# Another order of the DeltaNet projections, and the triangular inverses moved behind all of the preparation

## The chip, the cores and the metric

The kernel runs on one core of one Trainium2 chip. Its engines work side by side and wait for each other through semaphores: PE multiplies matrices, DVE, ACT and POOL work elementwise on 128 partitions, and SP issues most of the DMA transfers. The metric is the time of one execution on the device, in microseconds (us), and the median over several executions is what counts.

## The reference

One block of a bidirectional encoder, with 512 tokens and a model width of 1024. Two token mixers run in parallel on the same projection, a gated DeltaNet and a latent attention (MLA). Sigmoid gates merge them, and a mixture of 16 experts follows.

```python
proj = h @ w_in[l]
dn_qkv, dn_z, dn_b, dn_a, c_q, c_kv, k_r, gates = jnp.split(proj, split_at, axis=-1)
y_dn = gated_deltanet_branch(dn_qkv, dn_z, dn_b, dn_a, ...) @ w_o_dn[l]
y_mla = mla_branch(c_q, c_kv, k_r, ...) @ w_o_mla[l]
g_dn, g_mla = jnp.split(jax.nn.sigmoid(gates), N_BRANCHES, axis=-1)
x = x + gt1 * ((g_dn * y_dn + g_mla * y_mla) @ w_out[l])
...
# gated DeltaNet, once forwards and once backwards, 8 heads of 128, chunks of 64 tokens
qkv = jax.nn.silu(centred_depthwise_conv(qkv, conv_w))
q, k, v = jnp.split(qkv, 3, axis=-1)
lower = jnp.where(strict, jnp.einsum('bhnik,bhnjk->bhnij', k_beta, kc) * decay, 0.0)
t_inv = lax.linalg.triangular_solve(eye + lower, eye, left_side=True, lower=True, unit_diagonal=True)
u = t_inv @ v_beta
w = t_inv @ (k_beta * jnp.exp(gc)[..., None])
def step(state, xs):          # 8 steps, one behind the other
    v_new = u_i - w_i @ state
    o_i = qd_i @ state + intra_i @ v_new
    state = state * jnp.exp(gl_i)[..., None, None] + jnp.swapaxes(ks_i, -1, -2) @ v_new
```

## The kernel before, in words

The block runs in stages. Conditioning, the latents and the attention come first, then the DeltaNet part, which this text is about, then the output mixing and the router, and at last the experts, whose weights stream from DRAM.

Every projection of the DeltaNet is made by `proj_tiles`. One tile is one head, or 128 columns of the gates: 24 matmuls of 128x512, because each float32 product is split into high and low parts (`wh`, `wl`) and made as three. ACT makes the high parts and POOL subtracts for the low parts; every `lo_n`-th subtraction goes to DVE instead (L96). The weights come through four `wraw` buffers, which SP loads (L137), or ACT where `fill_q` says so.

The DeltaNet part has five pieces:

1. **Projections of keys and queries.** Each head goes through `conv` (one ACT operation, four on DVE at L660 and L662, then silu on ACT). The keys are also transposed to token order (`to_tok`: four transposes on PE into the one bank `tok`, a scaled copy on ACT into `tk`, a store). Between heads stand pieces of another, small product (`mod_g`).
2. **Decay blocks**, t = 0 to 3: POOL makes `gM`, PE the bank `pjb`, ACT the exponential `Dx`, POOL `Di`, DVE masks `Dx`. PE's products of keys with keys and queries (bank `gkq`) are multiplied into `nA` and `Di` by DVE (L761).
3. **Inverses.** `inverses(ty)`, once for each type of chunk, inverts 128 triangular blocks of 32x32 on DVE, one block in each partition: a run of 31 rows, and for row i a multiply of i*i elements (L783, `pr`) and a reduction (L784, `lanT`). The input goes through DRAM (`nd`) to `pr` and is copied to `nl`; the result goes through DRAM (`td`, `tt`) to `Tbd` and `TtC`.
4. **Projection of values**, written behind `inverses(0)`, each head followed by one tile of the gates' projection (`fill_g`).
5. **Eight steps.** `level(s)` loads a step's operands and completes the inverse by two small groups of products (bank `I`: `I<-TtC,Mb` and `I<-Tbd,Qb`). `step(s, L)` applies it to the values (bank `V`), passes the state `Sst` on (bank `S`) and writes the output. Steps 0 to 3 take type 0, steps 4 to 7 type 1. `inverses(1)` is written ahead of step 2, and DVE runs it behind `inverses(0)`. `fill_g` gives the rest of the gates' projection: a scheduler puts its matmuls where PE would wait, and what is left follows the last step.

The program is written in this order, and the scheduler fixes each engine's order at build time from dependences and priorities. Behind the steps the outputs `o` are normalised on DVE (L1024, L1032 scales), transposed on PE (bank `oT`) and multiplied by w_o_dn, beside the product of the attention's output (`am`) with w_o_mla.

Of the kernel before, what the change touches and what calls it, by code (L numbers as in the profile page):

```python
# [14 lines left out]
OP = mybir.AluOpType  # L15
# [25 lines left out]
def block_kernel(ctx: ExitStack, tc: tile.TileContext, x, c, positions, w_mod, b_mod, g_mix, w_in, conv_w,  # L41
# [87 lines left out]
    lo_eng, lo_n = [0], [3]  # L129
# [93 lines left out]
    p = bank("mm")  # L223
# [453 lines left out]

    for e, base, feat in ((0, 8, kf), (1, 0, qf)):
        for h, ps in proj_tiles(range(128 * base, 128 * base + 1024, 256)):
# [5 lines left out]
            if e == 0:  # L685
                pool.tensor_copy(feat[h], f)
            for _ in range(2):
                next(mod_g, None)
            sq = dp("sq", 512, bufs=4)
# [3 lines left out]
            sqs.append(sq)  # L693
            if e:
                sp.dma_start(kq_d.rearrange("t p (h n) -> p t h n", h=8)[:, :, h, :], kq[h].rearrange("p t s n -> p t (s n)"))
            if e == 0:
                to_tok(kc, 0, h)
                if h == 5:
                    decays()
            if h % 4 < 3:  # L700
# [33 lines left out]
    lanes_ap = lambda td, l0, n=16: td[l0:l0 + n, :].rearrange("l (j i) -> j l i", j=32)  # L734
    FT, FV = 0, 1
    for t in range(4):
# [31 lines left out]
    def inverses(ty):  # L768
# [4 lines left out]
        sp.dma_start(pr, nd_d[ty])  # L773
        dve.tensor_copy(nl[0:64], pr[0:64])
        dve.tensor_copy(nl[64:128], pr[64:128][:, ::-1])
        pool.memset(T, 0.0)
        pool.memset(T[:, 0:1024:33], 1.0)
        sq3 = lambda v: v.rearrange("p (a b) -> p a b", a=32)
        T3, n3 = sq3(T), sq3(nl)
        for i in range(1, 32):  # L780
            pv = pr[:, :i * i].rearrange("p (a b) -> p a b", a=i)
            nb = n3[:, 0:i, i][:, None, :].to_broadcast([128, i, i])
            dve.tensor_tensor(pv, T3[:, 0:i, 0:i], nb, op=OP.mult)  # L783
            dve.tensor_reduce(T3[:, 0:i, i], pv, axis=AX.X, op=OP.add)  # L784
        To, Tt = pr, nl
        dve.tensor_copy(To[0:64], T[0:64])
# [3 lines left out]
        sp.dma_start(td_d[ty], To)  # L790
        sp.dma_start(tt_d[ty], Tt)

    inverses(0)
    lo_n[0] = 6
    for h, ps in proj_tiles(range(2048, 3072, 256), to=lambda n: bank(n, 1, pp_)):
        sl = dp("sq", 512, bufs=4)
        for _ in range(0):
            next(mod_g, None)
        conv(ps, 16 + h, halves(sl))
        to_tok(sl, 1, h, ssq_k[:, :, h])  # L800
        for _ in range(FV):
            next(fill_g)
    pp_.close()
    wm.close()
    dp.close()
    if stop <= 1.5:
        return
    fill_q[0], lo_n[0] = act, 2

# [65 lines left out]
    def step(s, L):  # L875
# [24 lines left out]
        for g in range(2):  # L900
            hs = slice(4 * g, 4 * g + 4)
            pV = v4(bank("V", 1, ps_))
            for h in range(4):
                mm(pV[:, h, :], Tbd[:, 4 * g + h, :], vtok[:, 4 * g + h, :])
            if s < 7:
                v_ = vtok[:, hs, :]
                dve.tensor_tensor(v_, pV, bt[:, ty, t, hs][:, :, None].to_broadcast([128, 4, 128]), op=OP.mult)
            vn = dp("vn", [4, 128], bufs=2)
            for h in range(4):
                act.activation(vn[:, h, :], pV[:, h, :], AF.Copy, scale=col(beta, 4 * g + h))  # L910
            vns.append(vn)
        for g in range(2):
            if s < 7:
# [12 lines left out]
        for g in range(2):  # L926
# [8 lines left out]
            else:  # L935
                dve.tensor_tensor(Qs[g], pI, Qs[g], op=OP.add)
                pool.tensor_tensor(oo, oo, Qs[g], op=OP.add)

    L = level(0)
    for s in range(8):  # L940
        if s == 2:
            inverses(1)
        Ln = level(s + 1) if s < 7 else None
        step(s, L)
        L = Ln
# [712 lines left out]
```

## Time and profile before

| what | us |
|---|---|
| median of 3 runs (lowest, highest) | 1320.69 (1320.46, 1327.38) |
| the profiled execution | 1326.64 |
| its span in the trace | 1324.8 |

The span leaves out 1.84 us of the profiled execution's own time. PE is busy for 1241.3 us of the span, DVE for 689.0, ACT for 480.3 and POOL for 307.7. A time in a row below counts from the span's start. In the trace keys and queries take the stretch from about 218 to 347 us, the decay blocks lie around 347 to 378, the first inverse runs on DVE from 390.74 to 452.6, the second from 457.52 to 517, the steps end near 645, and the experts take the stretch from about 880 to 1310.

### The profile page before, as it was taken

The numbers are of one execution on the slowest core, as the hardware profiler recorded it, in microseconds if no ns is written. First come the engines' busy times: TensorE is split into PE (matmuls) and PEld (weight loads), VectorE is DVE, ScalarE is ACT, GpSimd is POOL, SyncE is SP. The second block draws the span as 40 slices with busy tenths as digits, with TensorE's granted clock in tenths as the row PEclk, the third lists the DMA queues.
The fourth block names the chain that finished last, engine by engine and source line by source line (L and its number), as shares of the span: only waits on it lengthen the run. The fifth ranks groups of instructions, "written<-read, shape, count | busy, mean of one in ns | idle before, by whom it ended". The sixth has DMA issues, their size and how long they took to land.

```text
span 1324.8 us, 18313 instructions
## 1 busy us (share of the span) xinstructions
PE 1241.3 (94%) x6933; PEld 775.3 (59%) x6933; DVE 689.0 (52%) x1312; ACT 480.3 (36%) x991; POOL 307.7 (23%) x259
## 2 busy tenths in 40 slices
PE   5999999999997987999999999699999999999895
PEld 2767777666676765877888777443443343343233
DVE  4587766365679996434587765501321312222125
ACT  4466655456643333444542326520210120120103
POOL 2321200233443451344222332310200020020003
PEclk9999999999998997999999999799999999999998
DMA  9521213744463466567579793599999999999995
GB/s 340 154 60 42 82 48 94 232 148 129 125 184 96 152 170 187 187 172 214 160 247 336 247 322 126 228 368 421 420 421 420 421 420 421 420 421 420 421 415 187
DMA packets 153507, 333.70 MB, mean 252 GB/s; under 512 B 44560, under 2 KB 104158, under 8 KB 128458
## 3 DMA queue, kind: packets, MB, share of 16 engines
q1 hardware_dynamic: 130048, 308.75, 63.6%
q10 hardware_dynamic: 23034, 23.36, 5.7%
q8 instruction: 55, 0.90, 0.3%
q0 software_dynamic: 336, 0.41, 0.1%
q14 instruction: 34, 0.28, 0.1%
HBM read 308.35 MB, written 24.13 MB: 251 GB/s over the span
## 4 chain that ended last, share of the span: by engine, by line
PE 67%; DVE 14%; DMA 10%; ACT 3%; issue 2%; POOL 1%; SPq 0%; DVEq 0%; ACTq 0%; POOLq 0%
PE mm L88 23%; PE wg L88 8%; PE wu L88 7%; PE dnp L88 6%; PE po L88 5%; DMA exw<-in_w_down_dram 3%; DVE pr L783 3%; PE sc L88 2%; DMA exw<-in_w_gate_dram 2%; PE I L88 2%; PE s L88 2%; PE pja L88 2%; DVE lanT L784 2%; DMA exw<-in_w_up_dram 2%; PE S L88 1%
## 5 line engine op out<-in xcount | busy, mean ns | idle before, releaser
L88 PE MATMUL mm<-hT,wh 128*128 128x512 f32 (+1 forms) x672 | 222.5, 408 | 0.0
L96 POOL TENSOR_TENSOR wl<-wraw,wh 128x512 fp32r<-128x512 f32 (+2 forms) x83 | 120.2, 1463 | 262.7 <-ACT wh L99 245.5
L88 PEld LDWEIGHTS mm<-hT,wh 128*128 128x128 f32 (+1 forms) x672 | 124.8, 189 | 44.2 <-issue 10.8
L99 ACT ACTIVATE wh<-wraw 128x512 fp32r<-128x512 f32 (+1 forms) x139 | 87.2, 650 | 139.7 <-PE mm L88 61.5
L88 PE MATMUL mm<-hT,wl 128*128 128x512 f32 (+1 forms) x336 | 135.7, 404 | 1.3 <-DVE wl L96 1.3
L88 PE MATMUL wg<-exw,xe 128*64 128x512 f32 x512 | 121.1, 600 | 3.6 <-DMA exw<-in_w_gate_dram 2.3
L88 PE MATMUL wu<-exw,xe 128*64 128x512 f32 x512 | 119.4, 605 | 1.5 <-DMA exw<-in_w_up_dram 1.5
L96 POOL TENSOR_TENSOR xl<-xs,xh 128x512 fp32r<-128x512 f32 x32 | 40.3, 1276 | 308.1 <-ACT xh L1358 308.0
L1515 DVE TENSOR_TENSOR ye<-dnp,gt 64x512 f32<-64x512 f32 x30 | 20.6, 688 | 133.4 <-PE dnp L88 117.4
L1456 DVE TENSOR_TENSOR xa<-sc,xa 128x512 f32<-128x512 f32 x56 | 38.5, 691 | 87.7 <-PE sc L88 87.7
L88 PEld LDWEIGHTS wu<-exw,xe 128*64 128x64 f32 x512 | 35.1, 138 | 66.4 <-issue 59.0
L88 PEld LDWEIGHTS mm<-hT,wl 128*128 128x128 f32 (+1 forms) x336 | 63.4, 189 | 16.8 <-DVE wl L96 1.7
L88 PEld LDWEIGHTS wg<-exw,xe 128*64 128x64 f32 x512 | 33.5, 136 | 64.7 <-issue 55.3
L96 DVE TENSOR_TENSOR wl<-wraw,wh 128x512 fp32r<-128x512 f32 (+1 forms) x56 | 47.7, 857 | 35.7 <-ACT wh L99 34.8
L783 DVE TENSOR_TENSOR pr<-lanT,nl 128x1 f32<-128x1 f32 (+30 forms) x62 | 57.5, 927 | 1.7
L88 PE MATMUL po<-W,am 128*128 128x512 f32 x192 | 50.1, 405 | 0.6 <-DVE W L96 0.6
L660 DVE SCALAR_TENSOR_TENSOR cv<-mm,vecT,cv 128x510 f32<-128x510 f32 (+1 forms) x32 | 23.9, 748 | 39.7 <-ACT cv L656 39.1
L88 PE MATMUL mm<-am,wh 128*128 128x512 f32 x128 | 40.8, 398 | 0.0
L88 PEld LDWEIGHTS po<-W,am 128*128 128x128 f32 x192 | 34.6, 188 | 10.4 <-issue 1.6
L88 PE MATMUL mm<-oz,wh 128*128 128x512 f32 x128 | 40.3, 397 | 0.0
L1581 POOL TENSOR_TENSOR xa<-xa,late 128x256 f32<-128x256 f32 (+1 forms) x16 | 10.7, 709 | 124.2 <-DMA late<-in_g_final_dram 124.2
L88 PE MATMUL mm<-OG,xh 128*128 128x256 f32 x128 | 34.1, 304 | 2.8 <-DVE OG L1367 2.8
(596 smaller groups left out, 2418.5 us busy)
## 6 DMA issues: line engine op xcount, KB each, us to landing
exw<-in_w_gate_dram SPq DMA_DIRECT2D x64, 1024.0 KB
exw<-in_w_up_dram SPq DMA_DIRECT2D x64, 1024.0 KB
exw<-in_w_down_dram SPq DMA_DIRECT2D x63, 1024.0 KB
wraw<-in_w_in_dram SPq DMA_DIRECT2D x38, 512.0 KB
wm<-in_w_mod_dram SPq DMA_DIRECT2D x32, 512.0 KB
wraw<-in_w_in_dram ACTq DMA_DIRECT2D x16, 512.0 KB
xa<-in_w_mod_dram SPq DMA_DIRECT2D x16, 512.0 KB
kq<-kq_d SPq DMA_DIRECT2D x7, 1024.0 KB
```

The source lines that it names most:

```text
L88: return pe.matmul(o, lhsT, rhs, start=start, stop=stop)
L96: eng.tensor_tensor(o, a, b, op=OP.subtract)
L99: act.activation(hi, src, AF.Copy)
L660: dve.scalar_tensor_tensor(cv[:, -s:], ps[:, :512 + s], w(d), cv[:, -s:], op0=OP.mult, op1=OP.add)
L783: dve.tensor_tensor(pv, T3[:, 0:i, 0:i], nb, op=OP.mult)
L784: dve.tensor_reduce(T3[:, 0:i, i], pv, axis=AX.X, op=OP.add)
L1456: dve.tensor_tensor(y[t][:, c:c + 512], ps, y[t][:, c:c + 512], op=OP.add)
L1515: dve.tensor_tensor(ye[o_, c], ps[64 * q:64 * q + 64, :], gt2[64 * q:64 * q + 64, c], op=OP.mult)
L1581: pool.tensor_tensor(y[t][:, cs], y[t][:, cs], gfin[:, cs], op=OP.mult)
```

## The change

The projections come in the order values, queries, keys. The eight value heads stay in the buffers of `Dx` and `Di` until they are transposed, since their scale comes from the keys. The transposes follow the keys, then the decay blocks, now with one gate tile (`FT`) behind each t. Only then comes `inverses(0)`, followed by ten more gate tiles, with every low part on POOL (`lo_n` 1000). There is one piece of `mod_g` for each head of values, queries and keys, where each key and each query had two. `kq_d` is stored in the keys' loop.

`inverses` becomes a generator that yields after each row. The input `nl` is now copied transposed, so that a row's operand lies contiguous in memory (`n3[:, i, 0:i]`), where it had steps of 128 bytes (`n3[:, 0:i, i]`). Of `inverses(1)` twelve rows come ahead of step 0. The rest comes in six portions, two in each of the steps 0 to 2, each issued behind the multiply that makes the step's `vtok`.

```diff
+    vals = []
+    for h, ps in proj_tiles(range(2048, 3072, 256)):
+        vals.append(dp("val", 512, bufs=4, tag=("Dx", "Di")[h % 2]))
+        conv(ps, 16 + h, halves(vals[h]))
+        next(mod_g, None)
+        if h == 5:
+            decays()
-    for e, base, feat in ((0, 8, kf), (1, 0, qf)):
+    for e, base, feat in ((1, 0, qf), (0, 8, kf)):
...
-            for _ in range(2):
-                next(mod_g, None)
+            next(mod_g, None)
...
-    FT, FV = 0, 1
+    FT = 1
+    for h in range(8):
+        to_tok(vals[h], 1, h, ssq_k[:, :, h])
     for t in range(4):
...
-        dve.tensor_copy(nl[0:64], pr[0:64])
-        dve.tensor_copy(nl[64:128], pr[64:128][:, ::-1])
+        sq3 = lambda v: v.rearrange("p (a b) -> p a b", a=32)
+        flip = lambda v: sq3(v).rearrange("p a b -> p b a")
+        dve.tensor_copy(sq3(nl)[0:64], flip(pr)[0:64])
+        dve.tensor_copy(sq3(nl)[64:128], flip(pr)[64:128][:, ::-1, ::-1])
...
-            nb = n3[:, 0:i, i][:, None, :].to_broadcast([128, i, i])
+            nb = n3[:, i, 0:i][:, None, :].to_broadcast([128, i, i])
             dve.tensor_tensor(pv, T3[:, 0:i, 0:i], nb, op=OP.mult)
             dve.tensor_reduce(T3[:, 0:i, i], pv, axis=AX.X, op=OP.add)
+            yield i
...
-    inverses(0)
-    lo_n[0] = 6
-    for h, ps in proj_tiles(range(2048, 3072, 256), to=lambda n: bank(n, 1, pp_)):
-        sl = dp("sq", 512, bufs=4)
-        for _ in range(0):
-            next(mod_g, None)
-        conv(ps, 16 + h, halves(sl))
-        to_tok(sl, 1, h, ssq_k[:, :, h])
-        for _ in range(FV):
-            next(fill_g)
...
-    fill_q[0], lo_n[0] = act, 2
+    lo_n[0] = 1000
...
+                done = dve.tensor_tensor(v_, pV, bt[:, ty, t, hs][:, :, None].to_broadcast([128, 4, 128]), op=OP.mult)
...
+            if s < 3:
+                with tc.issue_after(done.ins):
+                    upto_i(INV[s][g])
...
+    for _ in inverses(0):
+        pass
+    for _ in range(10):
+        next(fill_g)
+    fill_q[0], lo_n[0] = act, 2
+
+    INV, inv = ((18, 20), (23, 25), (28, 32)), inverses(1)
+
+    def upto_i(n):
+        while next(inv) < n:
+            pass
+
+    upto_i(12)
     L = level(0)
     for s in range(8):
-        if s == 2:
-            inverses(1)
```

The gates' projection has 24 tiles, so 576 matmuls. Before, 279 of them stand on PE ahead of the first step's products, 139 among the steps and 158 behind the last step. With the change 392 stand ahead of them: 86 between the last key's matmuls and the last `pjb`, then 306 in one run up to the first `I<-TtC`. 157 stand among the steps and 27 behind them.

Three places of the engines' orders follow. First PE at the end of the preparation, where `val` is a kept value head, `ident` the identity of a transpose, and `pja<-hT` is a matmul of a value projection. Before:

```order
L88 MATMUL gkq<-kq_2088 64x128 x2
L88 MATMUL pjb<-gM,Lbd_2045 128x512
L88 MATMUL pja<-hT_97,wh 128x512
L88 MATMUL pja<-hT_97,wl 128x512
L88 MATMUL pja<-hT_98,wh 128x512 x2
L88 MATMUL pjb<-gM,Lbd_2059 128x512
L88 MATMUL pja<-hT_98,wl 128x512
```

Of the change:

```order
L668 MATMUL tok<-ident,val 128x128 x4
L88 MATMUL pjb<-gM,Lbd_2045 128x512
L668 MATMUL tok<-ident,val 128x128 x8
L88 MATMUL pjb<-gM,Lbd_2059 128x512
L88 MATMUL gkq<-kq_2081 64x128 x2
L88 MATMUL gkq<-kq_2082 64x128 x2
L88 MATMUL gkq<-kq_2083 64x128 x2
L88 MATMUL gkq<-kq_2084 64x128
L668 MATMUL tok<-ident,val 128x128 x4
L88 MATMUL gkq<-kq_2084 64x128
```

The decay blocks stood among value projections; they now stand among the values' transposes, which write the one bank `tok` eight times, with 27 gate matmuls in between, all of them ahead of the third transposed head.

Second SP's queue around the first inverse, from just ahead of its load `pr<-nd` to the loads of its result. Before:

```order
L137 DMA wraw<-in_w_in_dram 128x4x256 x2
L773 DMA pr<-nd_2022 128x1024
L137 DMA wraw<-in_w_in_dram 128x4x256 x2
L771 DMA nd_2023<-nA_2034 32x16x32 x4
L137 DMA wraw<-in_w_in_dram 128x4x256 x8
L790 DMA td_2024<-pr 128x1024
L791 DMA tt_2026<-nl 128x1024
L773 DMA pr<-nd_2023 128x1024
L828 DMA TtC<-tt_2026 32x32x32 x4
```

Of the change:

```order
L137 DMA wraw<-in_w_in_dram 128x4x256 x2
L779 DMA pr<-nd_2022 128x1024
...
L137 DMA wraw<-in_w_in_dram 128x4x256 x2
L849 DMA ibd<-int_d 64x8x64 x2
...
L849 DMA ibd<-int_d 64x8x64 x2
L798 DMA td_2024<-pr 128x1024
L799 DMA tt_2026<-nl 128x1024
L779 DMA pr<-nd_2023 128x1024
L842 DMA Tbd<-td_2024 32x8x32
L827 DMA TtC<-tt_2026 32x32x32 x4
L842 DMA Tbd<-td_2024 32x8x32 x11
```

Two weight loads stand right ahead of `pr<-nd` as before, now of gate weights. Of the ten that stood between it and `td`, four are left (two of them between the `nd` stores that the dots leave out), and the loads of steps 0 and 1 stand there instead.

Third DVE at the first two steps, with `pr` and `lanT` the inverse's rows and `vtok` the hand on to the next step's state. Before:

```order
L783 TENSOR_TENSOR pr<-lanT,nl 128x961
L784 TENSOR_REDUCE lanT<-pr 128x31
L786 COPY pr<-lanT 64x1024
L787 COPY pr<-lanT 64x1024
L788 COPY nl<-lanT 64x1024
L789 COPY nl<-lanT 64x1024
L907 TENSOR_TENSOR vtok<-V,bt 128x512 x2
```

Of the change:

```order
L906 TENSOR_TENSOR vtok<-V,bt 128x512
L790 TENSOR_TENSOR pr<-lanT,nl 128x441
L791 TENSOR_REDUCE lanT<-pr 128x21
L790 TENSOR_TENSOR pr<-lanT,nl 128x484
L791 TENSOR_REDUCE lanT<-pr 128x22
L906 TENSOR_TENSOR vtok<-V,bt 128x512
L790 TENSOR_TENSOR pr<-lanT,nl 128x529
L927 TENSOR_TENSOR Sst<-Sst,S 128x4x128
L791 TENSOR_REDUCE lanT<-pr 128x23
L927 TENSOR_TENSOR Sst<-Sst,S 128x4x128
```

The whole second inverse stood ahead of the first `vtok`; its rows now stand between the steps' own operations.

## Rows read from the trace of the kernel before

**Rows 1.** The page: the chain that ended last, by engine.

```profile
PE 67%; DVE 14%; DMA 10%; ACT 3%; issue 2%; POOL 1%; SPq 0%; DVEq 0%; ACTq 0%; POOLq 0%
```

**Rows 2.** Busy time in stretches: PE, PEld, DVE, ACT, POOL, granted clock, DMA share, GB/s.

```profile
215.00:690.00 475.00, 447.90 (x3014) 336.30 (x3014) 307.48 (x571) 219.53 (x508) 167.72 (x137) 0.96 0.58 170
...
525.00:645.00 120.00, 118.01 (x1426) 97.12 (x1426) 52.89 (x111) 55.74 (x183) 46.53 (x39) 0.97 0.63 178
645.00:690.00 45.00, 45.00 (x202) 36.23 (x202) 31.43 (x82) 23.35 (x52) 13.38 (x10) 1.00 0.65 210
...
404.00:434.00 30.00, 23.26 (x93) 18.25 (x92) 29.27 (x36) 10.36 (x24) 11.29 (x8) 0.89 0.31 95
...
518.00:536.00 18.00, 17.94 (x156) 14.66 (x158) 1.58 (x3) 8.41 (x24) 1.11 (x2) 0.60 0.30 80
```

**Rows 3.** PE's waits, 360 to 545 us: total us, times, longest.

```profile
PE tok L668 <- ACT sq L663: 10.9, 4, 5.2
PE S L88 <- DVE vtok L907: 8.0, 1, 8.0
PE gkq L88 <- DVE Di L761: 2.2, 1, 2.2
```

**Rows 4.** PE's timeline: start, us, instruction, idle before it with its releaser.

```profile
403.39 0.63 PE L88 MATMUL mm<-hT,wh 128*128 128x512 f32 x2
...
404.10 0.64 PE L88 MATMUL pjb<-hT,wh 128*128 128x512 f32 x2
406.27 0.66 PE L668 MATMUL tok<-ident,sq 128*128 128x128 f32 x4 [1.54 <-ACT sq L663]
```

**Rows 5.** DVE's timeline in the two inverses; last the page's group of all 62 multiplies.

```profile
395.72 1.16 DVE L783 TENSOR_TENSOR pr<-lanT,nl 128x49 f32<-128x49 f32 x1
...
450.35 1.12 DVE L788 COPY nl<-lanT 64x1024 f32<-64x1024 f32 x1
...
457.52 0.69 DVE L774 COPY nl<-pr 64x1024 f32<-64x1024 f32 x1 [2.11 <-DMA pr<-nd]
...
464.29 0.26 DVE L783 TENSOR_TENSOR pr<-lanT,nl 128x49 f32<-128x49 f32 x1
464.58 0.21 DVE L784 TENSOR_REDUCE lanT<-pr 128x7 f32<-128x49 f32 x1
...
488.24 1.23 DVE L783 TENSOR_TENSOR pr<-lanT,nl 128x576 f32<-128x576 f32 x1
489.50 0.76 DVE L784 TENSOR_REDUCE lanT<-pr 128x24 f32<-128x576 f32 x1
...
L783 DVE TENSOR_TENSOR pr<-lanT,nl 128x1 f32<-128x1 f32 (+30 forms) x62 | 57.5, 927 | 1.7
```

**Rows 6.** SP's queue: issues with their start and length, and one wait.

```profile
452.61 0.34 SPq L791 DMA_DIRECT2D tt<-nl  x1
453.88 0.32 SPq L773 DMA_DIRECT2D pr<-nd  x1
467.24 19.39 SPq L828 DMA_DIRECT2D TtC<-tt  x4
...
SPq L828 <- DMA wraw<-in_w_in_dram: 29.2, 3, 13.0
```

**Rows 7.** ACT's timeline (one row), then groups by line: count, busy us, mean ns.

```profile
425.93 1.14 ACT L674 ACTIVATE tk<-tok,ssq_k 128x128 f32<-128x128 f32 x4 [0.68 <-PE tok L668]
...
L744 ACT ACT_TABLE_LOAD x2 | 2.6, 1283 | 0.0
...
L745 POOL TENSOR_TENSOR Di<-Dx,Mpk 128x512 f32<-128x512 f32 x6 | 8.5, 1422 | 1.2 <-ACT Dx L744 1.2
```

**Rows 8.** Groups on DVE behind the steps, 640 to 780 us.

```profile
L96 DVE TENSOR_TENSOR am<-a__6132,am 128x512 fp32r<-128x512 f32 x1 | 0.7, 693 | 1.5 <-ACT am L99 1.5
...
L1024 DVE SCALAR_TENSOR_TENSOR sqo<-o 128x128 f32<-128x128 f32 x24 | 7.4, 370 | 0.0
...
L1032 DVE TENSOR_TENSOR o<-o,ssq 128x1024 f32<-128x1024 f32 x4 | 6.8, 1768 | 0.0
```

More of the change, by code (lines that the diff above doesn't have):

```diff
@@ L693, in block_kernel @@
             sqs.append(sq)
-            if e:
+            if e == 0:
                 sp.dma_start(kq_d.rearrange("t p (h n) -> p t h n", h=8)[:, :, h, :], kq[h].rearrange("p t s n -> p t (s n)"))
-            if e == 0:
                 to_tok(kc, 0, h)
-                if h == 5:
-                    decays()
             if h % 4 < 3:
@@ L773, in inverses @@
         sp.dma_start(pr, nd_d[ty])
-        dve.tensor_copy(nl[0:64], pr[0:64])
-        dve.tensor_copy(nl[64:128], pr[64:128][:, ::-1])
+        sq3 = lambda v: v.rearrange("p (a b) -> p a b", a=32)
+        flip = lambda v: sq3(v).rearrange("p a b -> p b a")
+        dve.tensor_copy(sq3(nl)[0:64], flip(pr)[0:64])
+        dve.tensor_copy(sq3(nl)[64:128], flip(pr)[64:128][:, ::-1, ::-1])
         pool.memset(T, 0.0)
         pool.memset(T[:, 0:1024:33], 1.0)
-        sq3 = lambda v: v.rearrange("p (a b) -> p a b", a=32)
         T3, n3 = sq3(T), sq3(nl)
@@ L791, in inverses @@
         sp.dma_start(tt_d[ty], Tt)
-    inverses(0)
-    lo_n[0] = 6
-    for h, ps in proj_tiles(range(2048, 3072, 256), to=lambda n: bank(n, 1, pp_)):
-        sl = dp("sq", 512, bufs=4)
-        for _ in range(0):
-            next(mod_g, None)
-        conv(ps, 16 + h, halves(sl))
-        to_tok(sl, 1, h, ssq_k[:, :, h])
-        for _ in range(FV):
-            next(fill_g)
+        yield 32
     pp_.close()
@@ L906, in step @@
                 v_ = vtok[:, hs, :]
-                dve.tensor_tensor(v_, pV, bt[:, ty, t, hs][:, :, None].to_broadcast([128, 4, 128]), op=OP.mult)
+                done = dve.tensor_tensor(v_, pV, bt[:, ty, t, hs][:, :, None].to_broadcast([128, 4, 128]), op=OP.mult)
             vn = dp("vn", [4, 128], bufs=2)
```

## The prediction, before the result was known

> **What bounds the kernel now.** I read the chain of the last end first. PE holds 67% of it, DVE 14%, DMA 10% [rows 1], so the time is PE's work and the places where PE waits for DVE. Then the stretches. From keys to output mixing, 215 to 690 us, PE is busy for 447.90 of 475 us, which leaves 27.1 us idle at a mean granted clock of 0.96 [rows 2]. PE's waits say where: 10.9 us in four waits for a value head (`sq`) that the transposes need, 8.0 us in one wait of the state products for `vtok`, 2.2 us for `Di` [rows 3]. The first two have one cause. DVE runs the inverses beside the convolutions and ahead of the first `vtok`, so what PE needs stands in DVE's queue. A wait costs more than its length. After the 8.0 us one, PE is busy for all of 518 to 536 us at a granted clock of 0.60, between the two levels of 1.2 and 2.4 GHz, and around the value waits, 404 to 434, the mean is 0.89 [rows 2]. Behind the steps PE has no idle time: 45.00 of 45 us at 1.00 [rows 2], because 158 gate matmuls lie there.
>
> The experts' stream starts only when the mixing and the router are done. A microsecond won or lost between 215 and 690 us therefore goes to the end in full.
>
> **What goes.** Idle time: 27.1 us, of which some 2.5 us are short waits at places that stay (decays, `vn`), so 24.6. Slow clock: 18 us at 0.60 is 7.2 us lost, 30 us at 0.89 is 3.3, and the rest I put at 1.5, since 0.04 of 475 us is 19 us, an upper bound that counts idle stretches too [rows 2]: 12.0. Together **36.6 us**. PE's own work stays the same, 576 gate matmuls included; a matmul takes 0.236 us (three in 0.71 [rows 4]).
>
> **A shorter inverse.** From 49 to 576 elements the multiply grows by 0.97 us, or 1.84 ns an element, the reduction beside it by 0.55 us, or 1.04 ns [rows 5]. The multiply's operand has steps of 128 bytes, the reduction's input none. Contiguous, I take the reduction's rate. All squares from 1 to 31 are 10416 elements, so 0.80 ns each is 8.3 us; the input copies become strided like those of the result, 1.12 for 0.69 us [rows 5], two of them, minus 0.9. Gain: 7.4 us on DVE for each inverse; lower bound nothing, if the multiply is slow for its two inputs instead.
> The Trainium skill ("SBUF — State Buffer", Door 1: The DMA port swizzle) says that memory is read in 16-byte lines and a stride is free up to four float32. The 1.84 against 1.04 ns agree with it.
> Undisturbed, an inverse takes now about 47 us: multiplies 31 x 0.17 + 10416 x 1.84 ns = 24.4, reductions 15.8, copies 4.9, gaps 2. All 62 multiplies took 57.5 us [rows 5], 8.7 more than 2 x 24.4, so some 4.4 us for each inverse are disturbance. New: 47 - 7.4 + 4.4 = **44 us**.
>
> **The new end of preparation.** Eight transposes of values now pass through one `tok` bank: 0.66 us on PE [rows 4], then 1.14 us on ACT [rows 7], and the next may not start before. 27 gate matmuls lie between the first three, so two or three round trips are covered by them and some by `pjb` and `gkq`; I count two as bare, 2.4 us. ACT changes its function table on the way, twice 1.28 [rows 7], 2.6. The last decay chain (`Dx` on ACT, `Di` 1.42 on POOL [rows 7], masks on DVE) has nothing beside it for 3.2, estimated from its rows. Sum 8.2 idle, and 2 for the clock behind it, as around the value waits: **10.2 us**. Bounds: 2.2, what the wait for `Di` costs now [rows 3], and 14. Storing `kq_d` in the keys' loop and one `mod_g` piece fewer per head cost nothing: the projections' 24 matmuls per head (5.7 us) cover both; without that cover a store's issue would be some 0.4 us per head.
>
> **First inverse under 306 gate matmuls.** The run takes 306 x 0.236 = 72.2 us. The chain beside it: two weight loads stand ahead of `pr<-nd` on SP and wait for buffers, freed about 34 matmuls into the run, 8.0, and a split, so 10; `pr<-nd` to the copy 3.6 (453.88 to 457.52 [rows 5, 6]); inverse 44; `tt` to DRAM like that load, 3.6; issue of four `TtC` loads 1.9 and their landing 3.6. That is 66.7, ahead of PE by 5.5 us. I put **1 us** for it, 0 to 4.
> The price if SP is not free: before, `TtC` loads waited for weight loads, 29.2 us in three waits, and ended their issue at 486.63, 34.0 us after `tt` was issued [rows 6]. The change takes eight of those loads off SP's queue there, and I take the short end.
>
> **Steps 0 to 3 with portions of the second inverse.** Rows 13 to 31 are 9766 elements, at 2 x 1.05 ns and 0.4 us a row some 28 us, with input, copies and weights 32. DVE is busy for 52.89 of 120 us in the steps now [rows 2], so in the 79 us of steps 0 to 3 some 35 + 32 = 67 of 79 us: it fits, narrowly. The 8.0 us wait disappears, but each state sum and `vtok` may find a row in progress, at most 1.2 us for a multiply of 961. Six portions at 0.75: **4.5 us**, 0 to 9. The steps 4 to 7 need `TtC` of type 1 only some 14 us after the last portion; nothing for it.
>
> **Behind the last step.** Only 27 gate matmuls are left there, and 59 matmuls on `am` can follow before the transposes `oT`: 86 x 0.236 = 20.3 us of PE. DVE must by then have done `sqo` 7.4, 17 operations of 0.69 (splits of `am` and weights, products, sums) 11.7, and the scalings of `o` 6.8 [rows 8]: 25.9. The transposes come 5.6 us late, the first `am` split 1.5 us [rows 8], and the clock behind it 2.6, like around a wait of 5.2 us now. **9.7 us**, 3 to 13; before it was 0.
>
> **Sum.** 10.2 + 1 + 4.5 + 9.7 = 25.4 new against 36.6 gone: 11.2 us less. The profiled execution took 1326.64 us, its span 1324.8 and 1.84 around it, so it would be 1315.4. It stands 5.95 us above the median of 1320.69; the same difference from the median gives **1309.5 us**. About 0.5%, 6.6 us, is what a measurement of this kernel can tell from no change: 1314.1 to 1327.3.
>
> **Rivals.**
> 1. *The seams cost their upper bounds.* End of preparation 14, first inverse 4, portions 9, transition 13: 40 us, and nothing is won: 1324. For it: the value transposes did stall PE four times before, through ACT and DVE [rows 3]. Against it: those waits were for DVE, which is now idle there. No measurable change, 1314 to 1327. Chance 0.25.
> 2. *The scheduler's order hides the seams.* End of preparation 2.2, inverse 0, portions 4.5, transition 6: 12.7, so 1296.8. For it: 24 gate tiles give much freedom. Against it: few of them are left at either seam. 1296 to 1303. Chance 0.12.
> 3. *The other side: the first result's loads wait on SP as before.* With 34.0 us from `tt` to the last `TtC` issue [rows 6] in place of 5.5, the chain takes 95.2 us, 23 us more than the run of matmuls, and the stretch behind it runs slow, 7.2 us more [rows 2]: 1309.5 + 29 = 1338.7. Slower than can be measured once the chain is some 17 us longer than worked out: 5.5 us ahead, then 11.6 of stall, then the clock. For it: weight loads by ACT now fill the same buffers. Against it: SP's own queue is nearly empty there. Chance 0.08.
> 4. *The first inverse runs beside POOL's subtractions.* The change gives POOL all low parts. A multiply of 49 elements took 1.16 us beside POOL's work and 0.26 alone, the reductions 0.21 [rows 5]. If all 31 multiplies meet one, 28 us in place of 4.4 lie on the chain: 18 us of stall and 7 of clock, 1309.5 + 24 = 1333.7. At half of them it is 14 us, still 4 us late: 1313. From 22 us of disturbance on it is slower. Chance of that 0.05, since most low parts were POOL's before too, at 4.4 us.
> The Trainium skill ("GPSIMD Engine Reference", 1. Specifications) says the same as a rule: POOL shares its memory interfaces with DVE and contends with DVE instructions of two inputs. It speaks against giving POOL all of them; the 1.16 against 0.26 agree.
>
> **How the numbers follow.** As summed, 1303 to 1314: 0.50, likeliest, so 1309.5. Rivals 1 to 4: 0.25, 0.12, 0.08, 0.05. The range 1297 to 1327 leaves out rivals 3 and 4 and the edges, under 2 in 10; the forecast's own range is 1303 to 1314. Faster by over 0.5%: 0.50 + 0.12 = 0.62. Within 0.5%: 0.25. Slower: 0.13.
>
> **What would show it.** In the changed trace: multiplies of 576 elements near 0.77 us; no wait of transposes for `sq` and none of 8 us for `vtok`; PE's run of gate matmuls without a gap up to `I<-TtC`, and `TtC` issued within 10 us of `tt`; waits of a few us at `tok<-val` and at `oT`; a granted clock near 1.00 from 390 to 640 us. The prediction is wrong if PE waits more than 10 us at `I<-TtC`, if the multiply stays at 1.2 us, or if DVE is more than 95% busy in steps 0 to 3.

## The result, and the profile after

The changed kernel takes 1340.38 us (median of 4 runs, 1337.37 to 1341.41) where the kernel before takes 1322.6 in the same runs: a ratio of 1.0135, 95% interval 1.0106 to 1.0164. It is slower by some 18 us. The forecast was 1309.5, with a range of 1297 to 1327. The profiled execution took 1341.41 us, its span is 1339.5, which is 14.7 us longer than that of before. On PE that is 4.2 us more busy time and 10.5 us more idle time. The page's line of the changed kernel:

```profile
PE 1245.5 (93%) x6933; PEld 775.0 (58%) x6933; DVE 677.6 (51%) x1308; ACT 476.8 (36%) x988; POOL 307.9 (23%) x263
```

PE's waits in the changed kernel, with total, count and longest, answer to [rows 3].

```profile
PE mm L88 <- DVE wl L96: 12.4, 3, 8.6
...
PE gkq L88 <- DVE Di L767: 6.5, 3, 3.1
PE tok L668 <- ACT tk L674: 3.9, 3, 1.4
PE oT L1050 <- DVE o L1045: 3.4, 4, 1.7
PE pjb L88 <- ACT Dx L750: 2.8, 2, 1.8
```

Both old waits are gone, that for `sq` (10.9 us) and that of 8.0 us for `vtok`. Five others stand in their place: among the decay blocks (`gkq`, `tok`, `pjb`), for low parts of gate weights (`wl`), and behind the last step (`oT`). The stretches of the changed kernel, with the columns of [rows 2], show where they lie.

```profile
380.00:450.00 70.00, 56.75 (x319) 40.19 (x318) 30.94 (x56) 36.65 (x76) 27.41 (x24) 0.90 0.54 158
450.00:525.00 75.00, 66.38 (x276) 52.18 (x275) 57.80 (x82) 23.73 (x39) 39.98 (x33) 0.95 0.67 202
525.00:645.00 120.00, 114.75 (x1287) 90.81 (x1286) 78.35 (x151) 54.43 (x168) 44.36 (x40) 1.00 0.56 160
645.00:700.00 55.00, 50.22 (x439) 40.32 (x437) 35.80 (x100) 27.17 (x84) 17.73 (x13) 1.00 0.73 228
700.00:760.00 60.00, 56.36 (x247) 45.02 (x248) 49.41 (x64) 16.07 (x27) 13.16 (x8) 0.94 0.86 299
```

The first line holds the end of the preparation: 13.3 us idle at a clock of 0.90. The second holds the first inverse: 8.6 idle at 0.95. The third holds most of the steps, 5.3 idle at 1.00, where before [rows 2] had 2.0 idle but a stretch at 0.60. The fourth holds the end of the steps, which now lies near 676 us, and the transposes of the output, the fifth what follows them: 4.8 and 3.6 idle. Up to 677 us only 0.6 of that is idle. Before, there was none up to 690 [rows 2] and none behind it. The first line below is of the changed kernel, the second of before:

```profile
645.00:677.00 32.00, 31.37 (x364) 26.84 (x363) 15.39 (x33) 13.63 (x49) 10.49 (x9) 1.00 0.75 231
690.00:760.00 70.00, 70.00 (x308) 54.74 (x307) 54.68 (x66) 20.48 (x36) 19.32 (x13) 1.00 0.87 299
```

The mean clock of a stretch counts its idle time too. The slow time itself lies in three places of the changed kernel, each at a granted clock of 0.50, the level of 1.2 GHz:

```profile
424.80:438.50 13.70, 10.82 (x47) 7.01 (x46) 6.83 (x11) 7.72 (x14) 7.55 (x6) 0.50 0.56 133
517.00:523.80 6.80, 2.80 (x7) 2.23 (x8) 4.46 (x6) 0.00 (x0) 3.46 (x4) 0.50 0.60 193
701.30:708.10 6.80, 4.28 (x17) 3.15 (x16) 6.80 (x11) 1.26 (x2) 0.00 (x0) 0.50 0.84 301
```

PE is busy there for 10.8, 2.8 and 4.3 us. If it works at half its speed, as the levels say, these cost 5.4, 1.4 and 2.1 us; this is an estimate.

The end of the preparation as its own timeline shows it, on PE of the changed kernel (start, us, instruction, idle before it):

```profile
412.12 1.13 PE L88 MATMUL pjb<-gM,Lbd 128*128 128x512 f32 x2 [1.85 <-ACT Dx L750]
415.07 0.66 PE L668 MATMUL tok<-ident,val 128*128 128x128 f32 x4 [1.26 <-ACT tk L674]
418.29 1.09 PE L88 MATMUL gkq<-kq 128*64 128x128 f32 x14 [1.54 <-DVE Di L767]
422.52 0.66 PE L668 MATMUL tok<-ident,val 128*128 128x128 f32 x4 [1.32 <-ACT tk L674]
424.52 0.86 PE L668 MATMUL tok<-ident,val 128*128 128x128 f32 x4 [1.35 <-ACT tk L674]
429.07 3.68 PE L88 MATMUL gkq<-kq 128*64 128x128 f32 x32 [1.93 <-DVE Di L767]
...
446.58 2.09 PE L88 MATMUL gkq<-kq 128*64 128x128 f32 x32 [3.05 <-DVE Di L767]
```

Eight waits of 1 to 3 us (one of them in the lines left out) stand in 35 us: the round trips of the one `tok` bank and the chain `pjb`, `Dx`, `Di`, `gkq`, in turn. Then the first inverse on DVE of the changed kernel:

```profile
461.56 0.75 DVE L767 TENSOR_TENSOR Di<-gkq,Di 128x256 f32<-128x256 f32 x2
470.37 1.14 DVE L782 COPY nl<-pr 64x1024 f32<-64x1024 f32 x1 [8.07 <-DMA pr<-nd]
471.52 2.88 DVE L783 COPY nl<-pr 64x1024 f32<-64x1024 f32 x1
...
480.55 1.01 DVE L790 TENSOR_TENSOR pr<-lanT,nl 128x49 f32<-128x49 f32 x1
...
499.95 0.76 DVE L790 TENSOR_TENSOR pr<-lanT,nl 128x576 f32<-128x576 f32 x1
500.75 0.76 DVE L791 TENSOR_REDUCE lanT<-pr 128x24 f32<-128x576 f32 x1
...
519.18 1.03 DVE L797 COPY nl<-lanT 64x1024 f32<-64x1024 f32 x1
520.25 1.29 DVE L96 TENSOR_TENSOR wl<-wraw,wh 128x512 fp32r<-128x512 f32 x2
```

The row operand does what was forecast: 0.76 us for 576 elements, as the reduction beside it, where [rows 5] had 1.23. The Trainium skill ("SBUF — State Buffer", Door 1: The DMA port swizzle) has a stride free only within a 16-byte line; the 0.76 against 1.23 agree. But the inverse begins at 470.37, 79.6 us later than before, and two low parts of gate weights stand behind it on DVE. The next matmul in PE's order needs the first of them, so PE stands from 512.4 on and gets it at 521:

```profile
521.00 0.80 PE L88 MATMUL mm<-hT,wl 128*128 128x512 f32 x1 [8.59 <-DVE wl L96]
...
535.73 0.50 PE L88 MATMUL mm<-hT,wl 128*128 128x512 f32 x1 [1.96 <-DVE wl L96]
...
537.32 0.46 PE L88 MATMUL I<-TtC,Mb 128*32 128x32 f32 x32
```

One more thing shows in PE's own work. The pieces of `mod_g` keep their 64 matmuls but take 16.8 us of PE in place of 10.6. A timeline row and the page's group, first of before, then of the changed kernel:

```profile
240.41 1.06 PE L88 MATMUL mod<-wm,sil 128*32 128x512 f32 x8
L88 PE MATMUL mod<-wm,sil 128*32 128x512 f32 x64 | 10.6, 605 | 0.0
225.81 1.05 PE L88 MATMUL mod<-wm,sil 128*32 128x512 f32 x4
L88 PE MATMUL mod<-wm,sil 128*32 128x512 f32 x64 | 16.8, 605 | 0.0
```

Two pieces that stand side by side (eight matmuls) take as long as one alone (four), and in the changed kernel each stands alone.

### The profile page after: what moved, and what is told of

Its sections match the earlier page's. It is cut to its first block, busy times and chain, and to the rows that moved or that the text cites. A ratio compares the mean times of both kernels' runs of the same rounds, so it can differ in the third digit from the quotient of the medians.

```text
span 1339.5 us, 18333 instructions
## 1 busy us (share of the span) xinstructions
PE 1245.5 (93%) x6933; PEld 775.0 (58%) x6933; DVE 677.6 (51%) x1308; ACT 476.8 (36%) x988; POOL 307.9 (23%) x263
## 5 line engine op out<-in xcount | busy, mean ns | idle before, releaser
L88 PE MATMUL mm<-hT,wh 128*128 128x512 f32 (+1 forms) x800 | 261.2, 406 | 0.0
L96 POOL TENSOR_TENSOR wl<-wraw,wh 128x512 fp32r<-128x512 f32 (+2 forms) x87 | 122.9, 1425 | 285.7 <-ACT wh L99 262.2
L88 PEld LDWEIGHTS mm<-hT,wh 128*128 128x128 f32 (+1 forms) x800 | 148.6, 189 | 50.7 <-ACT wh L99 7.2
L88 PE MATMUL mm<-hT,wl 128*128 128x512 f32 (+1 forms) x400 | 162.3, 406 | 10.6 <-DVE wl L96 10.6
L88 PEld LDWEIGHTS mm<-hT,wl 128*128 128x128 f32 (+1 forms) x400 | 75.3, 188 | 32.8 <-DVE wl L96 11.4
L660 DVE SCALAR_TENSOR_TENSOR cv<-mm,vecT,cv 128x510 f32<-128x510 f32 (+1 forms) x48 | 35.9, 748 | 58.4 <-ACT cv L656 57.8
L96 DVE TENSOR_TENSOR wl<-wraw,wh 128x512 fp32r<-128x512 f32 (+1 forms) x52 | 41.7, 806 | 29.6 <-ACT wh L99 24.2
L790 DVE TENSOR_TENSOR pr<-lanT,nl 128x1 f32<-128x1 f32 (+30 forms) x62 | 43.2, 697 | 1.8
L88 PEld LDWEIGHTS po<-W,am 128*128 128x128 f32 x192 | 34.7, 188 | 10.4 <-issue 1.6
L662 DVE SCALAR_TENSOR_TENSOR cv<-mm,vecT,cv 128x511 f32<-128x511 f32 (+1 forms) x48 | 35.9, 749 | 1.4
```

What stands on the lines that cost most here:

```text
L88: return pe.matmul(o, lhsT, rhs, start=start, stop=stop)
L96: eng.tensor_tensor(o, a, b, op=OP.subtract)
L660: dve.scalar_tensor_tensor(cv[:, -s:], ps[:, :512 + s], w(d), cv[:, -s:], op0=OP.mult, op1=OP.add)
L662: dve.scalar_tensor_tensor(cv[:, :512 - s], ps[:, s:], w(d), cv[:, :512 - s], op0=OP.mult, op1=OP.add)
```

## The experiments

A seam is here a place where PE passes from one piece of the program to the next and may have to wait; cover is other, independent work that PE can do there. The theory after the result, called that of the seams: what the new order costs is cover. Before, the value projections (192 matmuls) lay under the first inverse and the gates' 576 were free for the rest. Now the whole chain from the last key to the output has only the gates' matmuls to hide under, and it got longer at its start. The row operand and the portions are no cause of the loss. Rivals: the portions slow the steps; DVE's low parts alone are the cause; the order costs nothing and a shorter inverse just moves a wait. Medians, and ratios to the kernel before with their intervals; in the runs marked * the scale of the values is left out, so they are no versions to use and only show where time goes:

| kernel | us | ratio |
|---|---|---|
| changed kernel | 1340.38 | 1.0135 (1.0106 to 1.0164) |
| before, contiguous rows | 1307.21 | 0.9893 (0.9867 to 0.9919) |
| before, rows and portions | 1306.12 | 0.9887 (0.9862 to 0.9911) |
| changed, strided rows | 1350.52 | 1.0211 (1.0185 to 1.0238) |
| changed, four more tiles' low parts on POOL | 1345.06 | 1.0171 (1.0146 to 1.0197) |
| changed, second inverse whole | 1342.75 | 1.0142 (1.0118 to 1.0166) |
| changed, no gate tile in the blocks | 1331.45 | 1.0061 (1.0039 to 1.0082) |
| changed, neither queue holds low parts back | 1336.33 | 1.0101 (1.0074 to 1.0128) |
| changed, values transposed at once * | 1323.17 | 1.0006 (0.9992 to 1.0020) |
| changed, these three together * | 1319.19 | 0.9973 (0.9959 to 0.9986) |
| changed, the first two together | 1330.07 | 1.0057 (1.0038 to 1.0076) |
| rows and portions, POOL takes the value stage | 1309.45 | 0.9909 (0.9888 to 0.9930) |
| rows and portions, no scale * | 1305.75 | 0.9877 (0.9855 to 0.9900) |
| three together, 64 matmuls kept back * | 1324.15 | 1.0012 (1.0001 to 1.0022) |
| two together, 64 kept back | 1333.41 | 1.0076 (1.0055 to 1.0096) |
| three together, 59 kept back, all low parts on POOL * | 1319.01 | 0.9968 (0.9950 to 0.9986) |
| two together, 64 kept back, all low parts on POOL | 1334.31 | 1.0096 (1.0079 to 1.0114) |

**One part alone, in the order of before.** The row operand only:

```diff
-        dve.tensor_copy(nl[0:64], pr[0:64])
-        dve.tensor_copy(nl[64:128], pr[64:128][:, ::-1])
+        dve.tensor_copy(sq3(nl)[0:64], flip(pr)[0:64])
+        dve.tensor_copy(sq3(nl)[64:128], flip(pr)[64:128][:, ::-1, ::-1])
...
-            nb = n3[:, 0:i, i][:, None, :].to_broadcast([128, i, i])
+            nb = n3[:, i, 0:i][:, None, :].to_broadcast([128, i, i])
```

> The kernel before with the contiguous row operand alone (order, portions and fill as before). Theory of the seams (the new order costs more at its seams than its cover is worth; the row operand is a gain by itself): both inverses get 7 to 8 us shorter, the 8.0 us wait for vtok falls below 2 us and most of the 7.2 us of slow clock behind it goes, the waits of the transposes shrink from 10.9 to 6 to 9 us: 1302 to 1311 us. Rival, the order was what mattered (a shorter inverse only lets PE wait for something else): 1318 to 1324 us.

And with the second inverse in portions, edited as in the change:

> The kernel before with the contiguous row operand and the second inverse in portions in the steps; the order of the projections, the decay blocks and the fill stay as before. Theory of the seams: as the one with rows alone or up to 6 us better, since the first vtok no longer stands behind the second inverse: 1298 to 1309 us. Rival, the portions slow the steps (a state sum waits for a row each time): 5 to 10 us above the one with rows alone.

Both came out in the theory's range: 1307.21 and 1306.12 us, clearly faster than before. PE's waits with rows and portions in the old order:

```profile
PE tok L668 <- ACT sq L663: 5.8, 4, 2.1
PE gkq L88 <- DVE Di L761: 2.2, 1, 2.2
...
PE S L88 <- DVE vtok L911: 1.1, 1, 1.1
```

and its stretch from keys to output, which has 13.7 us idle at a clock of 1.00, where before it was 27.1 at 0.96:

```profile
215.00:690.00 475.00, 461.31 (x3121) 347.69 (x3122) 311.94 (x600) 227.35 (x520) 165.47 (x141) 1.00 0.62 185
```

These are the waits that the change was forecast to remove, and the old order removes them too, without new ones. Rows alone give nearly all of it: the `vtok` wait falls from 8.0 to 2.2 us there. So from 1306 to 1340, some 34 us are the price of the order and of what goes with it, the lone pieces of `mod_g` among them. The other direction, the strided operand in the changed kernel:

> The changed kernel with the strided row operand of before (that alone undone). Theory of the seams: the first inverse, which nothing else of DVE interrupts, takes 8 us longer and PE waits that much longer ahead of the first step; a part of the longer second inverse shows in the steps: 1347 to 1355 us. Rival, that chain is not what PE waits for: within 3 us of 1340.

1350.52 us, 10 more. The first inverse takes 57.9 us there from its first copy to its last, where the changed kernel has 49.8, and PE's wait for the low part that stands behind it grew from 8.6 to 16.7 us by as much:

```profile
527.61 0.80 PE L88 MATMUL mm<-hT,wl 128*128 128x512 f32 x1 [16.70 <-DVE wl L96]
```

**Portions.** `upto_i(32)` ahead of `level(0)`, nothing in the steps:

> The changed kernel with the second inverse in one piece behind the first on DVE, not in portions. Theory of the seams: the portions are a gain in this order; the first vtok now waits for rows 13 to 31 and the copies of the second inverse, 30 us and more, of which few gate matmuls can cover anything: 1352 to 1372 us. Rival, the portions are what slows the steps: 1325 to 1338 us.

Neither theory had it right. It took 1342.75 us, which the intervals do not tell from the changed kernel. The portions are no cause of the loss, and no gain that can be measured: the first state products wait 6.0 us, not 30, since the scheduler itself puts `vtok` among the rows of an inverse that is written ahead of it.

```profile
551.65 2.08 PE L88 MATMUL S<-vtok,ktok 64*128 64x128 f32 x16 [6.03 <-DVE vtok L906]
```

**Low parts behind the first inverse.** Four more tiles with `lo_n` 1000, behind the ten:

```diff
-    fill_q[0], lo_n[0] = act, 2
+    fill_q[0] = act
+    for _ in range(4):
+        next(fill_g)
+    lo_n[0] = 2
```

> The changed kernel with four more gate tiles whose low parts all go to POOL, so that none of those ahead of the first step stands behind the inverse on DVE. Theory of the seams: PE runs through the gate matmuls and waits for TtC instead, for some 7 to 10 us: 1336 to 1342 us. Rival, the 8.6 and 2.0 us waits for DVE's low parts are the cause: 1327 to 1332 us.

It took 1345.06 us, outside both theories' ranges and within the intervals of the changed kernel, and the edit did not remove the wait: PE waits 8.6 us as before, now for POOL. POOL clears `lanT` for the second inverse, and that waits for the first inverse's last copy; POOL's timeline of the changed kernel shows the clearing already:

```profile
520.28 0.95 POOL L784 MEMSET lanT<- 128x1024 f32 x1 [15.89 <-DVE nl L797]
```

So in addition DVE clears for type 1 (`eng = dve if ty else pool`):

> The changed kernel with four more gate tiles whose low parts all go to POOL, and the clearing of the second inverse's result done by DVE, so that neither queue holds a low part back until the first inverse ends. Theory of the seams: the wait of 8.6 us for a low part goes, and PE waits for TtC instead, 5 to 9 us: 1336 to 1345 us. Rival, those waits are the cause: 1328 to 1332 us.

1336.33 us, 4 less than the changed kernel, though the two intervals overlap. PE was busy for 74.85 of the 75 us up to 525, so the wait itself is gone, and the wait for `TtC` that the theory put in its place did not come; but of its 10.6 us more than half are lost again. Between 645 and 690 PE is idle for 9.5 us, where the changed kernel has 4.8 between 645 and 700. No gate matmul is left behind the last step, where the changed kernel has 27. The longest single wait there, 5.0 us, is for ACT's first high part of `am`, with which the next product begins.

```profile
450.00:525.00 75.00, 74.85 (x318) 59.39 (x314) 58.60 (x82) 24.28 (x40) 43.47 (x33) 0.99 0.66 197
...
645.00:690.00 45.00, 35.51 (x365) 28.94 (x363) 30.09 (x85) 22.08 (x78) 16.42 (x11) 0.89 0.77 242
```

**The end of the preparation.** `FT = 0`, and 14 gate tiles behind the first inverse's start:

> The changed kernel with no gate tile among the decay blocks, and those four tiles behind the first inverse's start instead. Theory of the seams: gate matmuls are a fixed stock, so the blocks' idle time grows by some 4 to 9 us and the stretch under the first inverse gets as much more cover; the blocks' chain also gets shorter by the four tiles' work on ACT and POOL, two table loads of 1.28 us for each: 1330 to 1342 us. Rival, the gate tiles among the blocks carry the stretch: 1348 us and more.

1331.45 us, 9 less, near the low end of the theory's range. But the growth of the blocks' idle time by 4 to 9 us did not come: it is 11.3 us from 380 to 450, where the changed kernel has 13.3. The load `pr<-nd` goes out at 453.69 where the changed kernel has 462.21, and the copy begins at 457.80. So the gate tiles delayed the blocks more than their matmuls covered; that this comes from their work on ACT and POOL was not tested. This run also leaves 64 gate matmuls behind the last step in place of 27. Then `to_tok(vals[h], 1, h)` right behind `conv`, in place of the eight transposes behind the keys:

> The changed kernel with each value head transposed right behind its convolution, without the scale by the keys' norms, which this kernel leaves out. Theory of the seams: the eight transposes no longer lie on the chain from the last key to the first inverse; the decay blocks take 40 us in place of 58, their idle time falls from 13.3 to some 6 us, and the steps end earlier by that and leave more gate matmuls for the last seam: 1320 to 1330 us. Rival, the blocks are slow for another reason, or PE waits as long further on: 1337 to 1343 us.

1323.17 us, 17 less, the largest single part, in the theory's range. `pr<-nd` goes out at 447.33, and PE is busy for 68.24 of the 70 us that had 56.75:

```profile
380.00:450.00 70.00, 68.24 (x370) 48.87 (x369) 42.24 (x74) 41.97 (x62) 37.64 (x32) 1.00 0.52 150
```

The control without the scale in the old order took 1305.75 us against 1306.12, so leaving out the scale is no gain where the transposes lie off the path. In the changed order they lie on it, and without the scale one copy on ACT stands for four scaled ones. A run with the transposes behind the keys but without the scale was not made, so how the 17 us split between place and scale is not shown.

> Control for the runs without the scale: the kernel before with the contiguous row operand and the portions, and the values' transposes copied without the scale by the keys' norms, which this kernel leaves out. If the scale as such costs nothing on the path: within 3 us of 1306. If ACT's three more operations for each head count: 1298 to 1303 us.

**Together.**

> The changed kernel with all three seams taken away together: no gate tile among the decay blocks, no low part held back by the first inverse (POOL makes those of four more tiles, DVE clears the second inverse's result), and each value head transposed at once without the scale by the keys' norms, which this kernel leaves out. Alone they gave 9, 4 and 17 us. Theory of the seams: what the order costs is these seams, so together they give 20 to 30 us and the kernel comes near that with the order of before: 1309 to 1320 us. Rival, the order costs something more (values no longer cover the first inverse): 1320 to 1330 us.

> The changed kernel with no gate tile among the decay blocks and no low part held back by the first inverse; everything is computed. Theory of the seams: 9 and 4 us add up: 1325 to 1331 us. Rival, they are the same wait: 1331 to 1336 us.

1319.19 and 1330.07 us, the first at the edge between the two ranges. The three alone sum to 30 us, together they give 21, which fits one stock of matmuls under which all of them hide. Some 13 us to the control stay. In the trace of the three together PE has no idle time from 450 to 525 us, and 10.4 us from 645 to 690, at a clock of 0.92, where no gate matmul is left. More than half of that is one wait for the first high part of `am`; a run that loads `am` earlier was not made. The last line is of PE's waits from 645 to 700:

```profile
450.00:525.00 75.00, 75.00 (x381) 59.97 (x380) 60.67 (x98) 24.12 (x45) 39.81 (x31) 1.00 0.77 224
645.00:690.00 45.00, 34.55 (x221) 26.99 (x222) 36.75 (x98) 18.24 (x53) 9.06 (x6) 0.92 0.86 290
...
PE mm L88 <- ACT am L99: 5.6, 1, 5.6
```

The pages of the control and of the three together say that idle time is the smaller part of the rest:

```profile
PE 1233.4 (95%) x6933; PEld 768.7 (59%) x6933; DVE 670.7 (51%) x1312; ACT 475.7 (36%) x967; POOL 298.3 (23%) x259
PE 1240.7 (94%) x6933; PEld 772.1 (59%) x6933; DVE 670.3 (51%) x1304; ACT 474.6 (36%) x966; POOL 313.1 (24%) x267
```

The spans differ by 12.0 us, of which 7.3 are PE's busy time and 4.7 its idle time. PE is busy for 3.2 us more in the stretches at a clock of 0.50, which costs 1.6 us by the estimate above. The rest of the 7.3 is PE's own work, here too with `mod` at 18.9 us against 10.6, partly set off by the sums over squares (`pja<-sq,ones`), 10.1 against 13.4. No run with two pieces of `mod_g` side by side in the new order was made.

Would keeping some back for that place help? The tiles ahead of the steps go from 18 to 14:

> The run with three seams taken away (without the scale of the values, which this kernel leaves out), with 14 gate tiles written ahead of the steps in place of 18, so that 64 gate matmuls are left behind the last step where there were none. Theory of the seams: the steps start some 14 us earlier, the idle time and slow clock behind the last step (10.4 and 3.6 us) fall below 5 us, and that is most of what is left: 1306 to 1313 us. Rival, PE waits for the first inverse's result instead, or the order costs something more: 1316 to 1322 us.

> The changed kernel with no gate tile among the decay blocks, no low part held back by the first inverse, and 64 gate matmuls left behind the last step; everything is computed. Theory of the seams: as much better than its pair with none left: 1318 to 1326 us. Rival: the first inverse, which ends later here than without the values' transposes, leaves PE waiting for TtC: 1327 to 1333 us.

1324.15 and 1333.41 us, the first slower than its pair, the second not by its interval. But the edit did one thing more: DVE had a part of the low parts again, with 12.2 us of waits for them in the first. So the same with `lo_n` 1000 for all gate tiles:

> The run with three seams taken away (without the scale of the values, which this kernel leaves out), with 59 gate matmuls left behind the last step and all low parts of gate tiles on POOL. Theory of the seams: no wait for a low part ahead of the steps, and the last seam's 10.4 us idle and slow clock mostly gone: 1306 to 1314 us. Rival, gate matmuls kept back at one end are missed at the other (PE waits for TtC by as much as it gains), or the order costs something more: 1316 to 1322 us.

> The changed kernel with no gate tile among the decay blocks, all low parts of gate tiles on POOL and 64 gate matmuls left behind the last step; everything is computed. Theory of the seams: 1318 to 1326 us. Rival, as above: PE waits for TtC, whose inverse ends 11 us later here than without the values' transposes: 1327 to 1332 us.

1319.01 and 1334.31 us: nothing gained by the one, 4 us lost by the other. The rival was right for the first; the second is even above the rival's range. PE now waits for the first inverse's result, 4.5 us in the first run (and 5.9 in the second), and runs at 0.95 there, and the last stretch still has 5.8 us idle:

```profile
513.18 0.66 PE L88 MATMUL I<-TtC,Mb 128*32 128x32 f32 x32 [4.45 <-DMA TtC<-tt]
```

```profile
450.00:525.00 75.00, 69.50 (x424) 55.12 (x423) 61.82 (x107) 25.74 (x56) 38.15 (x31) 0.95 0.73 207
645.00:690.00 45.00, 39.24 (x206) 31.02 (x206) 31.37 (x88) 22.12 (x58) 11.65 (x9) 0.94 0.65 224
```

Gate matmuls that are kept for one end are missed at the other. That fits a shortage of cover in this order; a run that gave the chain other work to hide under, without changing the order, was not made. How the last 13 us split by cause is therefore not shown, only that PE's own work has a larger part in them than its idle time.

**Beyond both kernels.** Rows and portions in the old order, and all low parts of the value stage on POOL:

> The kernel before with the contiguous row operand, the second inverse in portions, and all low parts of the value stage on POOL instead of five in six. DVE loses some operations of 0.69 us that stand between rows and convolutions, so the remaining 5.8 us of waits for value heads shrink by 1 to 3 us; the rows meet POOL's work more often: 1302 to 1309 us.

1309.45 us, just above its range and 3 above the kernel without this edit; the intervals overlap, so which share is the better one is not shown. The fastest version of everything computed is the old order with rows and portions, 1306.12 us, 1.1% below before; rows alone are as fast within the intervals.

## Why the prediction was wrong, step by step

**What goes, 36.6 us: right as to the places.** Both waits went with the change. But in the old order with rows and portions the stretch's idle time falls by 13.4 us too, and its clock rises from 0.96 to 1.00. The account did not ask what each part of the change would win alone: some 14 us come from the contiguous rows alone, without the new order.

**A shorter inverse: right.** 0.76 us for 576 elements (0.77 forecast). All 62 multiplies take 43.2 us where they took 57.5, so 7.2 us for each inverse (8.3 forecast).

**The new end of preparation, 10.2 us: the first step that failed.** It measured 13.3 us idle and, by the estimate above, 5.4 us in clock: 18.7, beyond its bound of 14. I counted two bare round trips and one decay chain; the trace has three bare round trips, and waits for `Di` at three of the four decay blocks and for `Dx` at two. And I priced only PE's waits there. The same stretch also sets when the first inverse starts: `pr<-nd` goes out 15 us earlier with the values transposed at once and unscaled.

**First inverse under 306 matmuls, 1 us: the second step that failed.** It cost 10.6 us idle (8.59 and 1.96) and 1.4 us in clock, 12.0 in all, beyond its bound of 4. Counted from the last `pjb` at 451.98, `pr<-nd` went out at 462.21, as the 10 us said. The load then took 8.2 us (3.6 forecast) and the inverse 49.8 (44). The 3.6 came from the second inverse's load, which has no weight load right ahead of it; the prediction counted the two weight loads ahead of the first one as a wait for buffers, but not as work that lengthens the load behind them. The issue of the four `TtC` loads ended at 530.82, so 78.8 us after the start where 63.1 was forecast, and against a run of 72.2 us. The wait's place was not foreseen at all: not at `I<-TtC`, but at gate matmuls whose low part stands behind the inverse on DVE. Taking it away gave some 4 us, not clear of noise, and no gate matmul was then left behind the last step.

**Steps, 4.5 us: near in number, by luck.** They have 5.3 us idle up to 645, less the 1.96 us that belongs to the line above, and 0.6 up to 677: 3.9. The price was for waits at rows of the inverse on DVE. The trace has short waits there, most of them for ACT (`vn`, `Qb`, `o`), and hardly any for DVE.

**Behind the last step, 9.7 us: right.** 7.8 us idle from 677 to 760 and 2.1 us in clock: 9.9.

**PE's own work, put as unchanged: the third step that failed.** The prediction had it stay the same, and let one `mod_g` piece fewer per head cost nothing, since the projections' matmuls cover that. But PE has hardly any idle time where the pieces stand (busy for 111.64 of 112 us from 225 to 337), so their own time counts: 16.8 us for 10.6, 6.2 more. The sums over squares and a small product with ones gave back 3.7 of that (12.8 to 10.1 and 2.1 to 1.1). Over the whole span PE is busy for 4.2 us more, although it is busy for 5.7 us less in the stretches at a clock of 0.50 (29.2 us in place of 34.9), worth 2.8 us. So PE's own work grew by some 7 us, an estimate; what makes up the part that `mod` does not explain is not shown.

Sum with what was measured: 18.7 + 12.0 + 3.9 + 9.9 = 44.5 against 36.6, so 7.9 us more. The span grew by 14.7; the rest is PE's own work, the term that stood at nothing.

**What the prediction said would show it.** The multiply came near 0.77 us, the old waits for `sq` and `vtok` went, and waits at `tok<-val` and `oT` came. PE did not wait at `I<-TtC`. Its run of gate matmuls without a gap and a clock near 1.00 from 390 to 640 us did not come, and the issue of `TtC` ended 10.6 us behind `tt`. None of the three signs of being wrong came, so they did not cover the places where the time went.

**The rivals.** The third gave 1338.7, near the result, and for a wrong reason: the issue of `TtC` began 3.0 us after that of `tt` and ended 10.6 us after it, not 34.0. The fourth, the inverse beside POOL, holds in small: 49 elements took 1.01 us again, and the inverse was 5.8 us longer than forecast, not 24. The first, seams at their upper bounds, came nearest in mechanism: its 40 us were 44.5, but not at its places. Two of the four seams passed their bounds and the other two stayed below, and PE's own work it left unchanged too. None of them has the four stretches draw on one stock of 576 matmuls; that fits why the edits together gave 21 of 30 us and why matmuls kept back gained nothing. It does not explain the miss itself, since the sum took each stretch's matmuls rightly from the order: the chains beside them were longer than priced. The chance of 0.13 for a slower kernel was too low.

## What to carry to other kernels

Where one stock of independent work fills several gaps, price the gaps together: what fills one is missing in the next, so count the chain from end to end against the stock. Work that leaves the chain's cover (here 192 matmuls of value projections, some 45 us, moved ahead of it) is then lost stock; this last is argued, no run here tests it. A stretch of short round trips ahead of a long serial piece costs twice, once by PE's own waits and once by the later start. And of a change with several parts, ask for each what it would do in the old kernel: here one edit of the memory layout held nearly the whole gain. And work that is said to cost nothing, since something else covers it, costs its full time where its own engine has no idle time: look at what stands beside it in the order.

## What was not expected of the hardware

A load of the same tile took 8.2 us from issue to use at 462 us and 5.2 at 520.84 (the copy began at 526.04), where [rows 5, 6] have 3.6. The 8.2 stands right behind two weight loads on the queue; without them right ahead, in the run with no gate tile in the blocks, the same load took 4.1 us (453.69 to 457.80).

The transposing copy of 64x1024 elements took 1.14 us in one instruction and 2.88 in the next, which flips the other half, beside POOL's clearings and low parts. Multiplies of 16 to 49 elements, which take 0.2 us alone, took 1.0 to 1.15 each four times in a row. They lie from 476.61 to 481.56, beside POOL's subtractions for low parts (476.43 to 481.49); the reductions between them, with one input, took 0.17 to 0.19. With POOL idle, 144 elements took 0.31 at 484.13; beside the next subtraction (484.39 to 485.68), 169 took 1.06 at 484.81.

Two pieces of `mod` side by side on PE, eight matmuls of 128x512, took the same 1.06 us as four alone, 1.05. Why is not shown.
